# A hybrid decoder layer on one core: ACT and DVE issue ready work of the dense products before that of the mixers

## The chip, the cores and the metric

The kernel runs on one core of one Trainium2 chip. The metric is the device time of one execution in microseconds (us). Before the change the median of three runs is 1505.16 us (1505.06 to 1505.33). The engines are called PE (matrix products), PEld (its weight loads), DVE, ACT, POOL and SP (here SP issues all DMA transfers).

## What is computed

One decoder layer on 1024 tokens of width 1024, all in float32. The input is modulated, projected to 3984 columns, and the columns feed three groups of recurrent heads ("mixers"); their outputs are projected back, then comes a squared-ReLU MLP of width 4096. Cut to what matters:

```python
mod = silu(c) @ ada_w + ada_b                     # shift1, scale1, gate1, shift2, scale2, gate2
h = x * (1 + scale1) + shift1
z = h @ w_in                                      # 1024 x 1024 by 1024 x 3984
o_h = hgrn2_mixer(z_h, ...)                       # 4 heads, chunkwise gated linear attention
o_g = gla_mixer(z_g, ...)                         # 6 heads, the same with a low-rank gate
o_r = rwkv7_mixer(z_r, ...)                       # 6 heads, delta-rule recurrence
o = concatenate([o_h, o_g, o_r]) @ w_out          # 1024 x 1024
x = layer_norm(ALPHA * x + (1 + gate1) * o, ln1_g, ln1_b)
h = x * (1 + scale2) + shift2
m = square(relu(h @ mlp_w_up)) @ mlp_w_down       # 1024 x 4096, 4096 x 1024
x = layer_norm(ALPHA * x + (1 + gate2) * m, ln2_g, ln2_b)
```

## The kernel before, in words

**Blocks.** The tokens are cut into two blocks of 512 (`NB`, `NT`). `build` emits the work in this order: the input projection of block 0 (`z_block(0)`, `z_rest(0)`), the mixers of block 0 (`mix(0)`), the modulation's later sums (`ada_later`), the input projection of block 1 (`z_block(1)`, `z_rest(1)`), the output projection and layer norm of block 0 (`out_block(0)`), the last columns of block 1 (`z_last`), the MLP's input of block 0 (`mlp_moving`), the mixers of block 1 (`mix(1)`), eight MLP chunks of block 0 (`mlp_chunk`, 512 columns of the 4096 each; after the fifth of them stands `out_block(1)`), and eight of block 1, the last of them `mlp_last`.

**Dense products.** Each float32 operand is split in two float32r parts, high and low. For a weight slab of 128 rows, `slab` (L1282) loads it into a `raw` buffer, ACT casts it to `wh` (L1278 in `split`), and DVE subtracts to get `wl` (L1279). `mm3` (L1326) then issues three matmuls per pair of tiles (L1328 to L1330): high by high, high by low, low by high. This text calls one such matmul a product; there are 5040 of them. A slab gives 12 products in `prod_c` and `prod_t`, and four slabs can be held (`WB`). Results gather in the PSUM banks `dn` (pool `psd`, four of them) or later `tn` (pool `pst`), and ACT and DVE take them out: L1217 and L1218 (`shift`), L1373 and L1375 (`put`), L1478 and L1479 (`out_block`), L1499 to L1504 (squared ReLU), L1517 and L1519 (the MLP's sum). Buffers of the dense products lie in the pools `dp` and, once the mixers are over, `tp`.

**Mixers.** `mixers` runs over the four tiles of 128 tokens of a block. Each tile is a chain of small steps that alternates between DVE, ACT, PE and small transfers through DRAM: `rw_*` for the delta-rule heads (with `rw_invert`, L687 to L743, whose triangular inverses go through DRAM), `la_*` for the linear attention (`la_attn` L408 with seven levels of L417 to L438, `la_end`). Their buffers lie in the pools `mp` and `cp`, their PSUM banks `mr` and `ml` in `psm`. On PE there are 3219 issues that are not products, most of them of the mixers. The outputs go to DRAM (`oD`, L538 and L825), from where `out_block` reads them back (`from_dram` L1303, transposes L1293).

**Order.** No engine follows the order of the code. `Order` (L874) takes the recorded instructions, their dependences and buffers, and writes out one order per engine; `apply` fixes it, and on the chip each engine issues in that order, waiting where it must. `run` (L1016) plays the program through with costs by formula; when an engine is free, `pick` (L1059) chooses among the instructions that are ready by that play and whose new buffers fit (`fits`, L1050; buffers of one kind are given out in the order of the code). The choice is the lowest rank, which is the pair of a level (`self.level(n)` in `build` and `mixers`) and the place in the code. Levels: 0 for `mix(0)` and `out_block(0)`, 2 for `z_block(1)`, 3 for `ada_later`, 0, 0, 3.5, 4.5, 5.5, 6.5 for the steps of `mix(1)` (`M1`), 3, 4, 5 and so on for the MLP chunks. So within block 0 an instruction of the mixers that is ready goes ahead of one of `z_block(1)`. For PE alone `pick` has two rules ahead of the rank: products first while few columns have passed lately (`behind`, L1045), and staying in one tile mode of the array (L1078).

Of the kernel before, what the change touches and what calls it, by code (L numbers as in the profile page):

```python
# [831 lines left out]
PE, ACT, DVE, POOL, SP = ENGINES = ("PE", "Activation", "DVE", "Pool", "SP")  # L832
# [8 lines left out]

KEEP = 1.2

SWITCH, ISSUE = 130, 20
DMA_ISSUE, DMA_START, DMA_END = 500, 600, 900

# [27 lines left out]
class Order:  # L874
# [21 lines left out]
    def cost(self, n):  # L896
# [6 lines left out]
        if e == SP:  # L903
            k = 1
            for _, m in dst[0].ap:
                k *= m
            run = min(ap.ap[-1][1] if ap.ap[-1][0] == 1 else 1 for ap in (src[0], dst[0]))
            return k / run * max(0.44, max(4 * run, 512 if run > 16 else 0) / 360), 0
# [107 lines left out]
    def run(self):  # L1016
        n = len(self.ins)
# [10 lines left out]
        ready = {e: [] for e in ENGINES}  # L1028
# [12 lines left out]
        recent, self.sum = collections.deque(), 0  # L1041
        dense = [self.eng[k] == PE and self.ins[k].ins[0].bass_ap.dtype == F32R for k in range(n)]


        def behind():  # L1045
            while recent and recent[0][0] < t - HAM_TICK:
                self.sum -= recent.popleft()[1]
            return self.sum < KEEP * HAM_COLUMNS

        def fits(k):  # L1050
            want = {}
            for tag, name in (x for m in self.run_of.get(k, (k,)) for x in self.takes[m]):
                j = want.get(tag, 0)
                if used[tag] + j >= self.room[tag] or self.tags[tag][nxt[tag] + j] != name:
                    return False
                want[tag] = j + 1
            return True

        def pick(e):  # L1059
            held = []  # L1060

            def take(x):
                ready[e].remove(x)
                heapq.heapify(ready[e])
                return x[1]

            if e == PE and run:
                x = self.rank[run[0]]
                if x not in ready[e]:
                    return None  # L1070
                run.pop(0)
                return take(x)
            if e == PE and behind():
                for x in sorted(ready[e]):
                    if dense[x[1]] and fits(x[1]):
                        return take(x)

            if e == PE and self.now != (P, P):  # L1078
                for x in sorted(ready[e]):
                    if self.mode[x[1]] == self.now and fits(x[1]):  # L1080
                        run.extend(self.run_of.get(x[1], ())[1:])
                        return take(x)
            while ready[e]:
                k = heapq.heappop(ready[e])[1]
                if fits(k):
                    break
                held.append(k)
            else:
                k = None
            for x in held:  # L1090
                heapq.heappush(ready[e], self.rank[x])
            if e == PE and k is not None:
                run.extend(self.run_of.get(k, ())[1:])
            return k

        while done < n:
            for e in ENGINES:
                while idle[e] <= t:
                    k = pick(e)
                    if k is None:  # L1100
                        break
# [42 lines left out]
            t = events[0][0]  # L1144
            while events and events[0][0] <= t:
                _, what, k = heapq.heappop(events)
# [534 lines left out]
```

## Time and profile before

| | |
|---|---|
| median of 3 runs | 1505.16 us (1505.06 to 1505.33) |
| the profiled execution, its own time | 1511.53 us |
| its span, first to last instruction | 1509.7 us |
| PE busy | 1416.9 us, 94% of the span, 11226 matmuls |
| DVE busy | 1052.7 us, 70% |
| ACT busy | 708.0 us, 47% |
| DMA engines busy | 44.6% by the main queue |
| granted clock of TensorE, mean | 0.975 |

How to read it: the profiled execution is one execution with the profiler on. Times in the views are counted from the start of its span. Matmuls are pipelined: each is shown for some 0.39 us, and the next starts 0.23 us after it, so the distance of their starts is what counts. Idle time of PE is read with the wait that ended it. [...]

### The profile page before, as it was taken

The numbers are of one execution on the slowest core, as the hardware profiler recorded it, in microseconds if no ns is written. First come the engines' busy times: TensorE is split into PE (matmuls) and PEld (weight loads), VectorE is DVE, ScalarE is ACT, GpSimd is POOL, SyncE is SP. The second block draws the span as 40 slices with busy tenths as digits, with TensorE's granted clock in tenths as the row PEclk, the third lists the DMA queues.
The fourth block names the chain that finished last, engine by engine and source line by source line (L and its number), as shares of the span: only waits on it lengthen the run. The fifth ranks groups of instructions, "written<-read, shape, count | busy, mean of one in ns | idle before, by whom it ended". The sixth has DMA issues, their size and how long they took to land.

```text
span 1509.7 us, 29223 instructions
## 1 busy us (share of the span) xinstructions
PE 1416.9 (94%) x11226; PEld 1131.9 (75%) x11226; DVE 1052.7 (70%) x2130; ACT 708.0 (47%) x1527; POOL 25.4 (2%) x32
## 2 busy tenths in 40 slices
PE   6999998889899896989899999999999999999996
PEld 5878876667787675767677788787887888888884
DVE  8787479889785576979788765475569445445478
ACT  3543365677756544666657443323343323333331
POOL 1000000000000000000000000000000000000004
PEclk9999999999989997999999999999999999999998
DMA  9998662524424655142423243454336432333331
GB/s 349 331 340 290 191 191 68 164 80 142 125 86 131 197 171 190 51 133 69 122 80 89 67 153 94 143 182 155 91 93 217 144 96 93 97 93 97 94 116 56
DMA packets 163291, 214.00 MB, mean 142 GB/s; under 512 B 39856, under 2 KB 90192, under 8 KB 163152
## 3 DMA queue, kind: packets, MB, share of 16 engines
q1 hardware_dynamic: 163152, 212.14, 44.6%
q8 instruction: 88, 1.44, 0.4%
q14 instruction: 51, 0.42, 0.1%
HBM read 180.03 MB, written 32.06 MB: 140 GB/s over the span
## 4 chain that ended last, share of the span: by engine, by line
PE 47%; DVE 7%; ACT 3%; DMA 2%; issue 1%; POOL 1%; SPq 0%; DVEq 0%; ACTq 0%; POOLq 0%
PE dn L1330 10%; PE dn L1328 10%; PE dn L1329 10%; PE tn L1330 5%; PE tn L1329 5%; PE tn L1328 5%; DMA lnr<-in_ln_b_dram 1%; DVE wl L1279 1%; DMA G<-zgt 1%; PE ml L434 0%; ACT L154 0%; DVE Rs L423 0%; DVE xt L1462 0%; DVE ld L459 0%; PE tn L1293 0%
## 5 line engine op out<-in xcount | busy, mean ns | idle before, releaser
L1278 ACT CAST wh<-raw 128x512 fp32r<-128x512 f32 (+2 forms) x424 | 253.0, 599 | 538.2 <-PE dn L1330 253.3
L1279 DVE TENSOR_TENSOR wl<-raw,wh 128x512 fp32r<-128x512 f32 (+2 forms) x424 | 278.3, 661 | 303.1 <-ACT wh L1278 279.5
L1328 PE MATMUL dn<-wh,ah 128*128 128x512 f32 (+1 forms) x736 | 288.3, 395 | 10.1 <-ACT s L1373 3.4
L1329 PE MATMUL dn<-wl,ah 128*128 128x512 f32 (+1 forms) x736 | 289.9, 394 | 4.6 <-DVE wl L1279 4.6
L1330 PE MATMUL dn<-wh,al 128*128 128x512 f32 (+1 forms) x736 | 287.8, 396 | 4.5 <-DVE al L1504 4.5
L1328 PE MATMUL dn<-ah,wh 128*128 128x512 f32 x560 | 226.7, 406 | 18.6 <-ACT ah L1321 11.4
L1329 PE MATMUL dn<-al,wh 128*128 128x512 f32 x560 | 225.8, 403 | 0.0
L1330 PE MATMUL dn<-ah,wl 128*128 128x512 f32 x560 | 223.5, 402 | 0.9 <-DVE wl L1279 0.7
L1328 PEld LDWEIGHTS dn<-wh,ah 128*128 128x128 f32 x736 | 141.6, 193 | 42.2 <-ACT s L1499 5.2
L1330 PEld LDWEIGHTS dn<-wh,al 128*128 128x128 f32 x736 | 141.6, 193 | 33.2 <-DVE al L1504 6.6
L1329 PEld LDWEIGHTS dn<-wl,ah 128*128 128x128 f32 x736 | 142.3, 193 | 31.3 <-DVE wl L1279 5.3
L1328 PEld LDWEIGHTS dn<-ah,wh 128*128 128x128 f32 x560 | 106.5, 190 | 45.2 <-ACT ah L1321 11.4
L1330 PEld LDWEIGHTS dn<-ah,wl 128*128 128x128 f32 x560 | 105.7, 189 | 24.4 <-DVE wl L1279 2.0
L1329 PEld LDWEIGHTS dn<-al,wh 128*128 128x128 f32 x560 | 106.3, 190 | 22.5 <-issue 0.9
L1330 PE MATMUL tn<-ah,wl 128*128 128x512 f32 x256 | 100.8, 394 | 0.0
L1329 PE MATMUL tn<-al,wh 128*128 128x512 f32 x256 | 100.2, 391 | 0.0
L1328 PE MATMUL tn<-ah,wh 128*128 128x512 f32 x256 | 99.6, 389 | 0.0
L157 ACT ACTIVATE ld<-ld 128x320 f32<-128x320 f32 (+1 forms) x120 | 54.8, 489 | 25.7 <-DVE ld L417 17.5
L1519 DVE TENSOR_TENSOR xt<-xt,dn 128x512 f32<-128x512 f32 x104 | 64.4, 679 | 0.1
L1244 DVE SCALAR_TENSOR_TENSOR xt<-xt,xt 128x1024 f32<-128x1024 f32 x48 | 58.3, 1216 | 8.3 <-DMA xt<-in_ada_wt_dram 8.0
L1329 PEld LDWEIGHTS tn<-al,wh 128*128 128x128 f32 x256 | 48.1, 188 | 11.2
L1328 PEld LDWEIGHTS tn<-ah,wh 128*128 128x128 f32 x256 | 48.1, 188 | 10.6
(288 smaller groups left out, 1960.5 us busy)
## 6 DMA issues: line engine op xcount, KB each, us to landing
raw<-in_mlp_w_up_dram SPq DMA_DIRECT2D x128, 256.0 KB
raw<-in_mlp_w_down_dram SPq DMA_DIRECT2D x128, 256.0 KB
xt<-in_ada_wt_dram SPq DMA_DIRECT2D x48, 512.0 KB
raw<-in_w_in_dram SPq DMA_DIRECT2D x64, 256.0 KB
raw<-in_w_in_dram SPq DMA_DIRECT2D x48, 192.0 KB
raw<-in_w_out_dram SPq DMA_DIRECT2D x32, 256.0 KB
raw<-in_w_in_dram SPq DMA_DIRECT2D x32, 196.0 KB
raw<-in_xt_dram SPq DMA_DIRECT2D x24, 256.0 KB
```

The costliest lines, as they stand in the source:

```text
L157: ins = nc.scalar.activation(out, in_, func, **kw)
L1244: nc.vector.scalar_tensor_tensor(w, w, 1.0, self.cact, ALU.mult, ALU.mult, accum_out=self.sums[:, q:q + 1])
L1278: nc.scalar.copy(hi[:, 0:n], src)
L1279: (eng or nc.vector).tensor_tensor(lo[:, 0:n], src, hi[:, 0:n].bitcast(F32), ALU.subtract)
L1328: nc.tensor.matmul(ps, lh, rh, start=first, stop=False)
L1329: nc.tensor.matmul(ps, lh, rl, start=False, stop=False)
L1330: nc.tensor.matmul(ps, ll, rh, start=False, stop=last)
L1519: nc.vector.tensor_tensor(acc[t][:, cs], acc[t][:, cs], ps, ALU.add)
```

## The change

`Order.run` marks each instruction of ACT and DVE that writes or reads a buffer or bank of the pools `dp`, `psd`, `tp` or `pst` (`feeds`). When ACT or DVE is free, `pick` first takes the lowest-ranked marked instruction that is ready and fits, whatever its level; only if there is none does it choose by rank among the rest. Nothing is computed otherwise, and no buffer, tile or transfer is added or removed. The orders of PE, POOL and SP are made by the same rules as before, but follow, since what becomes ready when in the play changes.

```diff
--- before.py
+++ after.py
@@ -841,6 +841,8 @@
 
 KEEP = 1.2
 
+DENSE = ("dp", "psd", "tp", "pst")
+
 SWITCH, ISSUE = 130, 20
 DMA_ISSUE, DMA_START, DMA_END = 500, 600, 900
 
@@ -1041,6 +1043,9 @@
         recent, self.sum = collections.deque(), 0
         dense = [self.eng[k] == PE and self.ins[k].ins[0].bass_ap.dtype == F32R for k in range(n)]
 
+        feeds = [self.eng[k] in (ACT, DVE) and any(t.split("_")[-2] in DENSE for t, _ in self.uses[k])
+                 for k in range(n)]
+
 
         def behind():
             while recent and recent[0][0] < t - HAM_TICK:
@@ -1064,6 +1069,10 @@
                 heapq.heapify(ready[e])
                 return x[1]
 
+            if e in (ACT, DVE):
+                for x in sorted(ready[e]):
+                    if feeds[x[1]] and fits(x[1]):
+                        return take(x)
             if e == PE and run:
                 x = self.rank[run[0]]
                 if x not in ready[e]:
```

Lines of the classes below stand nine further down in the changed kernel: L1278 becomes L1287, L1293 becomes L1302.

The order on ACT, around the casts of four slabs of `z_block(1)` (`wh_1032` to `wh_1041`, L1278 and L1287). Before, they stand in the mixers' last tile (tile 3: `ld_746`, `ld_752`, `sm_734`), and between two casts come five to ten other instructions:

```order
L1278 CAST wh_1032_5796<-raw_1031_5794 128x392
L157 ACTIVATE ld_746_4447<-ld_746_4447 128x5x64
L782 COPY UV_670_3873<-mr_735_4351 64x3x64
...
L157 ACTIVATE ld_749_4467<-ld_749_4467 128x10x32 x2
L1278 CAST wh_1035_5814<-raw_1034_5812 128x392
L517 COPY sc_1631<-ml_748_4454 64x6x64
...
L777 COPY sm_738_4382<-mr_737_4375 128x192
L157 ACTIVATE ld_752_4487<-ld_752_4487 128x20x16 x2
```

After, they stand in tile 2 (`ld_678`, `wk_631`), with two or four instructions between them:

```order
L1287 CAST wh_1032_5796<-raw_1031_5794 128x392
L157 ACTIVATE wk_627_3508<-wk_625_3501 128x384
L580 ACTIVATE wk_631_3522<-wk_610_3434,oka_1627,vcols_524 128x128
L1287 CAST wh_1035_5814<-raw_1034_5812 128x392
L580 ACTIVATE wk_631_3522<-wk_610_3434,oka_1627,vcols_524 128x128 x2
L1287 CAST wh_1038_5832<-raw_1037_5830 128x392
L1382 COPY s2_1023_5778<-dn_995_5630 128x392
L157 ACTIVATE ld_678_3901<-ld_678_3901 128x5x64
```

The same casts have moved up by about one tile of the mixers.

The order on PE at the end of `mix(0)`. Before, its last issue (L497) stands among the products of `z_block(1)`, and the 96 products of `z_rest(1)` are still to come ahead of `out_block(0)`:

```order
L1329 MATMUL dn_5792<-wl_5887,ah_4968 128x392
L497 MATMUL ml_4709<-V_4181,ld_4693 64x64 x10
L1330 MATMUL dn_5792<-wh_5886,al_4969 128x392
...
L1264 MATMUL ml_4751<-consts,mod 8x128
L1328 MATMUL dn_5950<-ah_4843,wh_5956 128x512
```

After, the last product of `z_rest(1)` (`dn_5953`) stands ahead of the last two of the five small levels of tile 3's `la_attn` (L434), and no product comes until `out_block(0)` transposes what it read back (L1302):

```order
L1339 MATMUL dn_5953<-ah_5018,wl_6083 128x512
L434 MATMUL ml_4581<-Rs_4579,ld_4574 32x32 x20
L434 MATMUL ml_4610<-Rs_4608,ld_4603 32x32 x20
L446 MATMUL ml_4632<-Qz,K_4180 32x64 x20
L471 MATMUL ml_4671<-st,ld_4659 128x128
...
L497 MATMUL ml_4709<-V_4181,ld_4693 64x64 x10
L1273 MATMUL ml_4751<-consts,mod 8x128
...
L1302 MATMUL dn_6112<-consts,raw_6110 128x128 x4
```

The dense work of block 1's projection, which ran beside the whole of `mix(0)` and past its end, now ends before `mix(0)` does: 99 issues of mixers and modulation stand without a product between them.

## Rows read from the trace of the kernel before

**Rows 1.** The page: busy time of each engine, share of the span, instructions.

```profile
PE 1416.9 (94%) x11226; PEld 1131.9 (75%) x11226; DVE 1052.7 (70%) x2130; ACT 708.0 (47%) x1527; POOL 25.4 (2%) x32
```

**Rows 2.** Stages: start:end, length, busy (instructions) by engine, granted clock, DMA, GB/s.

```profile
203.00:470.00 267.00, 245.39 (x3524) 190.81 (x3524) 218.29 (x527) 178.67 (x453) 0.00 (x0) 0.96 0.39 119
470.00:607.00 137.00, 119.04 (x574) 92.74 (x573) 87.18 (x178) 67.04 (x132) 1.86 (x2) 0.90 0.58 179
607.00:890.00 283.00, 264.15 (x3581) 202.63 (x3581) 236.71 (x536) 176.29 (x432) 0.00 (x0) 0.98 0.29 86
```

**Rows 3.** The same view of a stretch with products alone.

```profile
1178.00:1444.00 266.00, 266.00 (x1153) 216.18 (x1151) 126.23 (x197) 85.94 (x144) 0.00 (x0) 1.00 0.32 98
```

**Rows 4.** Waits of PE, 203:470: waiting line, releaser, us, times, longest.

```profile
PE dn L1328 <- DVE s L1218: 4.5, 4, 2.5
...
PE dn L1328 <- ACT s L1373: 1.4, 1, 1.4
```

**Rows 5.** Timeline of ACT, 389:408: start, us, engine, line, operation, names, shapes, count.

```profile
390.70 0.52 ACT L1278 CAST wh<-raw 128x392 fp32r<-128x392 f32 x1
...
404.47 0.51 ACT L1278 CAST wh<-raw 128x392 fp32r<-128x392 f32 x1
```

**Rows 6.** The view of rows 2 for two stretches around it.

```profile
395.00:408.00 13.00, 9.23 (x63) 8.30 (x63) 6.72 (x15) 11.89 (x31) 0.00 (x0) 0.99 0.62 167
408.00:425.00 17.00, 17.00 (x223) 14.13 (x223) 8.98 (x21) 8.36 (x22) 0.00 (x0) 0.50 0.31 95
```

**Rows 7.** Waits of PE, 607:890.

```profile
PE dn L1328 <- ACT s L1499: 2.1, 2, 1.3
...
PE dn L1330 <- DVE al L1504: 1.7, 3, 1.3
```

**Rows 8.** Timeline of DVE, 441:465, the end of the mixers of block 0.

```profile
440.88 0.81 DVE L423 TENSOR_TENSOR Rs<-ld,Qz 128x640 f32<-128x640 f32 x1
...
445.47 0.56 DVE L1279 TENSOR_TENSOR wl<-raw,wh 128x392 fp32r<-128x392 f32 x1
...
448.77 1.04 DVE L1279 TENSOR_TENSOR wl<-raw,wh 128x392 fp32r<-128x392 f32 x2
...
454.07 1.04 DVE L1279 TENSOR_TENSOR wl<-raw,wh 128x392 fp32r<-128x392 f32 x2 [1.47 <-ACT wh L1278]
...
459.78 0.68 DVE L1279 TENSOR_TENSOR wl<-raw,wh 128x512 fp32r<-128x512 f32 x1
462.93 0.83 DVE L537 TENSOR_TENSOR o<-o,ms 128x640 f32<-128x640 f32 x1
```

**Rows 9.** Timeline of SP, 462:505: the mixers' last store and a read-back.

```profile
463.78 0.33 SPq L538 DMA_DIRECT2D oD<-o  x1
...
498.11 0.36 SPq L1305 DMA_DIRECT2D raw<-oD  x1
```

**Rows 10.** Timeline of SP, 889:893: the same pair for block 1.

```profile
890.03 0.33 SPq L538 DMA_DIRECT2D oD<-o  x1
...
892.33 0.38 SPq L1305 DMA_DIRECT2D raw<-oD  x1
```

**Rows 11.** Chain that ended last, in order of time: a transfer in it.

```profile
659.82 5.03 DMA G<-zgt
```

**Rows 12.** Timeline of PE, 500:509: the first products of the output projection.

```profile
508.11 1.22 PE L1328 MATMUL dn<-wh,ah 128*128 128x512 f32 x2 [1.40 <-ACT wh L1278]
```

**Rows 13.** Waits of PE, 470:607.

```profile
PE dn L1293 <- DVE s L1300: 5.9, 2, 4.8
PE dn L1329 <- DVE wl L1279: 4.6, 1, 4.6
```

**Rows 14.** Waits of ACT, 203:470 (first row) and 607:890.

```profile
ACT wh L1278 <- PE dn L1330: 8.2, 7, 4.4
...
ACT wh L1278 <- PE dn L1330: 33.3, 16, 3.4
```

**Rows 15.** Timeline of ACT, 413:437: one such wait.

```profile
419.64 0.52 ACT L1278 CAST wh<-raw 128x392 fp32r<-128x392 f32 x1 [4.42 <-PE dn L1330]
```

## The prediction

> **What bounds the kernel now.** I read the page first. PE is busy for 94% of the span, DVE for 70%, ACT for 47% [rows 1], so PE sets the time, and what a change in order can give lies in the remaining 6% and in stretches at the lower clock. Where products run alone, 1153 of them take 266 us [rows 3]: 0.231 us each, with nothing lost. From 890 us on the kernel looks like that, and the built order of PE is the same before and after for the last 2368 issues. Up to 203 us the input projection of block 0 fills PE, and product 860 comes after 67 other issues in both orders. So only three stages can move [rows 2]: 203 to 470 (mixers of block 0 beside the projection of block 1), 470 to 607 (output projection, layer norm), 607 to 890 (mixers of block 1 beside MLP chunks). In the first, 600 products at 0.231 are 139 us; the other 128 us go to 1484 other issues, so one of these costs 0.087 us with its waits.
>
> The view of waits says why PE stands still in the first stage. Its products wait for what takes banks empty: 4.5 us for DVE's L1218 and 1.4 for ACT's L1373 [rows 4]. [...] ACT casts a weight slab at 390.70 and the next at 404.47 [rows 5], while it is busy with mixers for 11.89 of 13 us; PE is busy for only 9.23 of these 13, and the clock is 0.50 for the 17 us behind [rows 6]. A slab is 12 products, 2.8 us of PE; 13.8 us without one starves it. This is the spot that the change aims at.
>
> **The change part by part.** Nothing is added or removed; instructions move. All counts here are of the built orders.
>
> *Feeding PE in the first stage, a gain.* With casts and emptied banks ahead of the mixers, the products' waits (5.9 us) should nearly all go: I take 5. Of the 21 us at the low clock at most half, 10.5, can come back, since PE was busy in the large piece; part of that piece was mixers, which wait for DVE at either clock. I take 7. Sum 12, bounds 0 (the low clock only moves) and 16.4.
>
> *The same in the third stage.* [...] I take 7, bounds 0 and 9.3.
>
> *The end of the mixers of block 0, a cost.* Before, product 1392, the last of z_block(1), comes after all 1545 issues up to the mixers' last, and the 96 products of z_rest(1) (22 us) cover the way from the mixers' last store to the output projection. After, all 96 are issued while 90 of these issues are still to come, and nothing is left to cover that way. How long is it? From the end of the third small level's Rs at 441.7 to the mixers' store at 463.78 is 22.1 us [rows 8, 9]; DVE's L1279 in it takes 3.3, casts and products between the steps some more, so I take 17 (13 to 22). Store to read-back: 2.3 us, the gap that block 1 shows [rows 10]. The transfer: 5 us, the length of one on the chain [rows 11], 3 at best. From the sixth read-back, which must wait until a first `raw` buffer is free, to the first product it was 10.0 us [rows 9, 12]. Together 34 us (28 to 41). In that time PE has 99 issues and 32 transposes, 131 at 0.087 or 11 us. It loses 23 (17 to 30). Before, PE is idle for 18 us of the second stage [rows 2], and 10.5 of these lie elsewhere in it [rows 13]; of the other 7.5 I count 5 at this place, one piece of them the 1.4 us of [rows 12]. The low clock behind the gap is there already, 0.90 over the stage [rows 2]. Net cost: 18 by these middles; I take 15, nearer the low end, because DVE and ACT work for the mixers alone there, and keep 12 and 25.
>
> *Steps that stay behind.* Before, PE had made 1611 other issues when out_block(0) began; after it is 1555, so 56 issues of block 1's first tile, 4.9 us, come later, together with the DVE steps in front of them. They fall to where PE waits for the layer norm and its slab, 5.9 and 4.6 us [rows 13]. I take a gain of 2, bounds 0 and 4.9. DVE's later sums for the modulation go ahead of mixers too, at 60 to 160 us, and cost nothing: products of block 0 cover them, and PE's place in the mixers is the same at product 860.
>
> *The end of the mixers of block 1.* They end at product 2634 instead of 2449, with 102 products (23.6 us) behind them before out_block(1). Their way to its transposes is some 12 us: the 2.3 of [rows 10], the 5 of [rows 11], and a handful of DVE and ACT steps the size of L537's 0.83 [rows 8], say 5. So it is covered, with 11 us to spare, and costs nothing; were the cover gone, it would cost what block 0's end costs.
>
> *Sum.* -12 - 7 + 15 - 2 = -6 us on the profiled execution's own 1511.5 us, so 1505.5. That execution is 6.4 us above the median of the runs; taken off the median, 1505.2 - 6 = **1499**.
>
> **The rivals.** *Starved at the output projection (slower).* If DVE's dense work delays the mixers themselves, the gap grows. DVE is busy for 218 of 267 us in the stage [rows 2]. The 102 dense splits of z_block(1) and z_rest(1) that go ahead are about 60 us at 0.52 to 0.68 us each [rows 8]; before, 94 of them ran when the mixers left DVE free. If half of that time now stands in the chain, the store comes at 463.8 + 30 = 494 and the first product of out_block(0) 17 us later, at 511 instead of 508; with 56 issues (4.9) still owed and the third stage gaining nothing, the time is up by 8, at two thirds by 18. I put it at 1518, between the two. It decides at a first product later than 508. For it speaks how far the mixers lag: at product 1360 the order has 1095 other issues behind it, not 1535. Against it: DVE's idle 49 us in the stage take up some.
>
> *A cast that waits holds the mixers behind it (slower).* ACT issues in order. Its casts already waited for PE to free a `wh` buffer: 8.2 us in the first stage, 33.3 in the third [rows 14], 4.4 of it in one place [rows 15]. Before, they stood where the mixers had little ready; now ready steps stand behind them. If that much comes again in front of mixers, block 0's end is 8.2 us later (-6 + 8 = +2), and block 1's 33, of which 11 are covered: 22 more lost, +24. I put it at 1518, halfway between. [...]
>
> *No difference.* In the third stage the casts wait for PE, not PE for them, so products are fed already; gains and cost cancel: 1505.
>
> *A larger gain.* All clock and waits return and the gap is at its low bound: -16 - 9 + 12 - 5 = -18, or 1487.
>
> That the rule does nothing is out: the casts stand a tile earlier in the order.
>
> **How the numbers follow.** About 0.2%, 3 us, is what a measurement of this kernel can tell from no change. Forecast (1490 to 1502) 0.42, larger gain 0.08, no difference 0.18, starved 0.20, held casts 0.12. So faster 0.50, same 0.18, slower 0.32. The range reaches from the larger gain's 1487 to just above the slower cases' middle, 1520; the outer halves of these two, about 0.14, and what lies under 1487 are left out. The faster cases alone span 1487 to 1502.
>
> **What would show it.** Right: in the stage from 203 us no stretch at the low clock before the products run out; no 14 us between two casts; a gap of 28 to 41 us between the last product of z_rest(1) and the first of out_block(0) with the low clock in it; that first product at 495 to 506; the mixers of block 1 ending some 40 us later than 890, and products at 0.231 us on both sides of out_block(1). Wrong: a first product of out_block(0) later than 508, PE waiting for transposes near product 2736, or ACT's waits for PE at L1287 well above those of [rows 14] with the mixers' steps late behind them.

## The result, and the profile after

The changed kernel takes 1483.7 us (median; 1482.9 to 1487.0), against 1505.2 us for the kernel before on the same chip: ratio 0.985, 95% interval 0.983 to 0.987. It is faster by 21.5 us. The prediction was 6 us, with a range that ended at 1487: the sign was right, the size was more than three times too small.

The page of the changed kernel, busy time by engine, against [rows 1]: the work is the same, and PE is busy 11 us less.

```profile
PE 1406.1 (95%) x11226; PEld 1124.2 (76%) x11226; DVE 1055.1 (71%) x2130; ACT 708.9 (48%) x1527; POOL 25.4 (2%) x32
```

To compare kernels, I cut each trace at the same three products, whose order is the same in all of them: the first of `z_block(1)`, the first of MLP chunk 0 and the first of `out_block(1)`. The stretches are called start, first part (it holds the mixers of block 0, the gap behind them and the output projection) and MLP part (the mixers of block 1 beside MLP chunks). For the changed kernel, in the columns of [rows 2]; the first part is two rows, cut at the first product of `out_block(0)`:

```profile
0.00:209.00 209.00, 187.76 (x916) 156.91 (x917) 150.05 (x320) 88.23 (x182) 4.17 (x12) 0.98 0.84 283
209.00:502.40 293.40, 270.46 (x3651) 212.56 (x3649) 227.76 (x540) 192.57 (x475) 0.00 (x0) 0.95 0.43 129
502.40:591.40 89.00, 80.53 (x412) 64.14 (x412) 62.96 (x110) 40.34 (x73) 1.87 (x2) 0.94 0.59 184
591.40:930.00 338.60, 330.10 (x3915) 255.28 (x3914) 287.35 (x644) 212.75 (x508) 0.00 (x0) 1.00 0.37 106
930.00:1485.20 555.20, 537.27 (x2339) 435.34 (x2337) 326.99 (x520) 175.00 (x291) 19.37 (x18) 0.99 0.37 116
```

The kernel before, cut at the same products:

```profile
0.00:203.40 203.40, 187.44 (x916) 157.15 (x916) 147.38 (x318) 87.50 (x182) 4.17 (x12) 0.98 0.86 291
203.40:508.10 304.70, 278.66 (x3753) 215.55 (x3752) 241.37 (x589) 200.57 (x506) 0.00 (x0) 0.96 0.42 125
508.10:600.70 92.60, 79.07 (x326) 62.96 (x326) 57.42 (x101) 39.08 (x67) 1.86 (x2) 0.89 0.61 192
600.70:956.30 355.60, 335.95 (x3897) 261.00 (x3896) 278.89 (x605) 205.71 (x483) 0.00 (x0) 0.98 0.32 97
```

The start is 5.6 us longer, the first part 14.9 shorter (397.3 to 382.4), the MLP part 17.0 shorter, the rest 1.8 longer. The first part's figure flatters: that execution of the kernel before lay 6.4 us above its median, and six kernels below that have the same order there (runs 2, 5, 6, 7, 9 and 12) take 389.5 to 391.2 us. Against their mean, 390.4, the first part won 8.0.

The MLP part won most. Its length minus PE's busy time is PE's idle time: 355.60 - 335.95 = 19.65 before, 338.60 - 330.10 = 8.50 after, so 11.2 of the 17.0 us; the other 5.9 are busy time, at a clock of 1.00 instead of 0.98. (In the traces of these two kernels the granted clock is 1.00 or 0.50, and products of 512 columns start 0.43 us apart at 0.50 (before, 509.98 to 512.97 us) and 0.23 at 1.00. The low clock means 0.50 throughout.) Of the idle time, 14.3 us stood ahead of issues of the mixers and 5.3 ahead of products before; 4.9 and 3.6 after. Waits of PE in this part of the changed kernel, the three largest (the first and third are products, compare [rows 7]):

```profile
PE dn L1337 <- ACT ah L1511: 1.8, 2, 1.5
PE ml L488 <- DVE o L480: 1.7, 3, 0.6
PE dn L1337 <- DVE xt L1528: 1.2, 1, 1.2
```

Around the end of block 0's mixers it went as described. The store and the first read-back on SP (compare [rows 9]), then the first products of the output projection on PE (compare [rows 12]):

```profile
486.62 0.34 SPq L538 DMA_DIRECT2D oD<-o  x1
...
488.82 2.57 SPq L1314 DMA_DIRECT2D raw<-oD  x5
```

```profile
464.88 0.40 PE L1339 MATMUL dn<-ah,wl 128*128 128x512 f32 x1
...
502.39 0.96 PE L1337 MATMUL dn<-wh,ah 128*128 128x512 f32 x3 [0.34 <-ACT wh L1287]
```

The last product of `z_rest(1)` starts at 464.88, so 37.5 us pass without a product; forecast 34 (28 to 41). The stretch, and the piece of it at the low clock; the view counts 223 matmuls where the prediction counts 131 issues, because most issues of the mixers show as two matmuls in the trace (some 190 for the 99; the 32 transposes show as 32):

```profile
465.30:502.40 37.10, 22.23 (x223) 18.01 (x223) 18.12 (x34) 19.68 (x46) 0.00 (x0) 0.59 0.50 154
468.20:495.50 27.30, 17.94 (x166) 14.85 (x166) 10.75 (x22) 14.14 (x35) 0.00 (x0) 0.50 0.39 113
```

And the casts of slabs on ACT in the projection of block 1 (compare [rows 5], where two are 13.8 us apart): the longest distance between two casts there is now 10.3 us, between these two, and the next longest 7.5.

```profile
419.03 0.62 ACT L1287 CAST wh<-raw 128x512 fp32r<-128x512 f32 x1
...
429.36 0.61 ACT L1287 CAST wh<-raw 128x512 fp32r<-128x512 f32 x1
```

### The profile page after: what moved, and what is told of

The parts are those of the page before. It is cut to its first block, busy times and chain, and to the rows that moved or that the text cites. A ratio compares the mean times of both kernels' runs of the same rounds, so it can differ in the third digit from the quotient of the medians.

```text
span 1485.2 us, 29273 instructions
## 1 busy us (share of the span) xinstructions
PE 1406.1 (95%) x11226; PEld 1124.2 (76%) x11226; DVE 1055.1 (71%) x2130; ACT 708.9 (48%) x1527; POOL 25.4 (2%) x32
## 4 chain that ended last, share of the span: by engine, by line
PE 51%; DVE 4%; DMA 3%; ACT 2%; issue 1%; POOL 1%; SPq 0%; DVEq 0%; ACTq 0%; POOLq 0%
PE dn L1339 11%; PE dn L1338 11%; PE dn L1337 10%; PE tn L1338 5%; PE tn L1337 5%; PE tn L1339 5%; DMA lnr<-in_ln_b_dram 1%; PE ml L434 1%; DVE wl L1288 1%; DMA zht<-s 1%; DMA x1D<-xt 0%; DMA G<-zgt 0%; PE mr L598 0%; ACT wh L1287 0%; DVE xt L1471 0%
## 5 line engine op out<-in xcount | busy, mean ns | idle before, releaser
L1287 ACT CAST wh<-raw 128x512 fp32r<-128x512 f32 (+2 forms) x424 | 253.5, 599 | 500.4 <-PE dn L1339 215.9
L1337 PE MATMUL dn<-wh,ah 128*128 128x512 f32 (+1 forms) x736 | 284.6, 390 | 8.5 <-ACT s L1382 3.9
L1339 PE MATMUL dn<-wh,al 128*128 128x512 f32 (+1 forms) x736 | 283.4, 390 | 3.8 <-DVE al L1513 3.8
L1338 PEld LDWEIGHTS dn<-al,wh 128*128 128x128 f32 x560 | 105.8, 189 | 22.2 <-issue 0.5
L1253 DVE SCALAR_TENSOR_TENSOR xt<-xt,xt 128x1024 f32<-128x1024 f32 x48 | 58.4, 1220 | 14.6 <-DMA xt<-in_ada_wt_dram 14.5
L1339 PEld LDWEIGHTS tn<-ah,wl 128*128 128x128 f32 x256 | 48.2, 188 | 11.2
```

The costliest lines, as they stand in the source:

```text
L1253: nc.vector.scalar_tensor_tensor(w, w, 1.0, self.cact, ALU.mult, ALU.mult, accum_out=self.sums[:, q:q + 1])
L1287: nc.scalar.copy(hi[:, 0:n], src)
L1337: nc.tensor.matmul(ps, lh, rh, start=first, stop=False)
L1338: nc.tensor.matmul(ps, lh, rl, start=False, stop=False)
L1339: nc.tensor.matmul(ps, ll, rh, start=False, stop=last)
```

## The experiments

All start from the changed kernel, except the seventh. Where a rule holds for a part of the code alone, `self.at` has the place in the code at which that part begins: "ada" for `ada_later`, "z1" for `z_block(1)`, "zr1" for `z_rest(1)`, "out0" for `out_block(0)`, "mlp" for the first MLP chunk. The table has all of them; in the texts quoted below the MLP part is sometimes called the MLP stage or the third stage. "Without a product" is the longest time between the starts of two products in the MLP part, except the 5 to 6 us of the transposes ahead of `out_block(1)`, which all have. The lengths are those of one profiled execution each. The runs were timed on several chips; each ratio is to the kernel before on the same chip.

| kernel | start | first part | MLP part | PE idle in it at mixers, at products | without a product | median us | ratio to before (95%) |
|---|---|---|---|---|---|---|---|
| before | 203.4 | 397.3 | 355.6 | 14.3, 5.3 | 11.3 | 1505 to 1506.5 | 1 |
| changed | 209.0 | 382.4 | 338.6 | 4.9, 3.6 | 3.8 | 1483.7 | 0.983 to 0.987 |
| 1 ahead of the MLP | 207.5 | 384.8 | 363.0 | 16.0, 5.9 | 11.8 | 1509.4 | 1.001 to 1.004 |
| 2 MLP only | 203.8 | 390.9 | 336.1 | 3.4, 1.4 | 2.8 | 1486.0 | 0.985 to 0.987 |
| 3 ACT only | 205.6 | 397.4 | 349.2 | 10.2, 4.4 | 8.6 | 1506.2 | 0.999 to 1.001 |
| 4 DVE only | 208.0 | 373.9 | 342.9 | 6.7, 3.6 | 3.5 | 1480.1 | 0.981 to 0.984 |
| 5 DVE's splits, MLP | 203.9 | 389.8 | 356.5 | 10.7, 6.7 | 11.2 | 1504.3 | 0.997 to 1.001 |
| 6 DVE's others, MLP | 205.4 | 391.2 | 358.2 | 14.4, 4.7 | 12.5 | 1513.0 | 1.003 to 1.006 |
| 7 mixers later | 202.5 | 389.5 | 354.4 | 14.8, 2.5 | 13.8 | 1505.4 | 0.997 to 1.000 |
| 8 DVE, no modulation | 201.4 | 373.7 | 341.5 | 5.6, 3.9 | 3.5 | 1475.4 | 0.977 to 0.982 |
| 9 DVE's rows broken | 203.1 | 390.9 | 339.8 | 6.8, 4.0 | 4.5 | 1490.3 | 0.988 to 0.991 |
| 10 as 8, and ACT in the MLP | 203.5 | 373.5 | 342.3 | 5.6, 3.2 | 3.6 | 1475.8 | 0.978 to 0.982 |
| 11 as 10, products kept | 201.7 | 381.9 | 336.0 | 4.9, 1.4 | 7.0 | 1479.7 | 0.981 to 0.985 |
| 12 PE's order alone | 202.4 | 390.0 | 366.5 | 5.2, 20.0 | 5.0 | 1514.5 | 1.004 to 1.007 |

**1 and 2: which part of the program.**

```diff
         feeds = [self.eng[k] in (ACT, DVE) and any(t.split("_")[-2] in DENSE for t, _ in self.uses[k])
+                 and k < self.at["mlp"]
                  for k in range(n)]
```

> The rule holds only for instructions ahead of the MLP in the code. Of the 24.5 us between the two profiled executions, 17.0 lie between the start of the first MLP chunk and out_block(1). If the stages add, this kernel keeps the 11.3 and 3.6 us won ahead of the MLP and the 5.6 lost at the start, and has the third stage of before: about 9 us below before, 1494 to 1499 us, third stage 353 to 358 us. Rival (one shift carries through: what block 1's mixers had not issued early is what fills the third stage): the third stage is shortened here too, under 347 us, and the time is below 1490.

The second has `k >= self.at["mlp"]` in that place.

> The rule holds only for instructions of the MLP chunks and later. If the stages add: start and first stage as before (203 and 305 us), third stage 336 to 342 us instead of 355.6, the time 1486 to 1491 us, below the changed kernel if its 5.6 us at the start are real. Rival (the third stage's gain needs the later start of block 1's mixers): third stage over 347 us, time over 1495.

The MLP part of the first, then of the second, in the columns of [rows 2]:

```profile
592.30:955.30 363.00, 341.12 (x3915) 265.19 (x3913) 286.95 (x643) 214.34 (x507) 0.00 (x0) 0.97 0.33 98
```

```profile
594.70:930.80 336.10, 331.25 (x3897) 257.07 (x3897) 280.64 (x605) 204.85 (x483) 0.00 (x0) 0.99 0.35 102
```

The MLP alone gives 20 of the 21.5 us, with the first part and the start as before. Ahead of the MLP the rule won 6 us in the first part, but lost 4 at the start, and the MLP part behind it became 7 us longer than 356 (the mean of the kernel before and of runs 5 to 7, which gain nothing there: 355.6, 356.5, 358.2, 354.4). So the first run, 3 us slower than before, bears out neither line of its expectation: the parts don't simply add. Why the MLP part grew isn't settled. Its idle time is 2 us above that of before and its clock 0.97.

**3 and 4: which engine.**

```diff
+                 and self.eng[k] == ACT
```

> The rule holds on ACT alone. My prediction's reading (late casts on ACT starve the products) wants at least half of the gain here: 1495 us or less. Rival (DVE's share decides, since the low part of a slab is a DVE step and PE's order hardly moves by ACT's rule): within 3 us of before, 1502 to 1508, with the waits of PE in the third stage near 19 us as before.

> The rule holds on DVE alone. If ACT's late casts were the cause: 1495 to 1505 us, and gaps of over 10 us between two casts in the first stage as before. If DVE's share decides: 1481 to 1490 us, PE idle in the third stage 8 to 11 us instead of 19.7, products up to 468 us without a stretch at the low clock.

ACT's share alone gives nothing that can be measured in the time, DVE's alone all, and 4 to 5 us more than both (3.6 by the medians, 4.8 by the ratios). The idea that late casts on ACT are the main cause is out. By parts ACT's rule isn't quite without effect: the MLP part is 7 us shorter than 356, but the first part 7 longer than 390.4. The latter has some 42 us at the low clock in that execution, as much as the profiled execution of the kernel before, so it may be scatter. The MLP part, for ACT alone and for DVE alone:

```profile
603.00:952.20 349.20, 334.67 (x3897) 259.80 (x3896) 279.51 (x605) 205.65 (x483) 0.00 (x0) 0.98 0.34 99
```

```profile
581.90:924.80 342.90, 332.58 (x3913) 256.97 (x3911) 285.29 (x638) 209.55 (x497) 0.00 (x0) 0.99 0.35 102
```

PE's waits with ACT alone, 14.5 us, are below the 19 that were expected, at a time that is the same; and even with ACT's rule two casts of the MLP part are 18.9 us apart, so it isn't ACT's choice that holds them up. With DVE alone the distance between two casts in the first part went up to 19.9 us once, with no more than 4.8 us without a product anywhere in the projection; a piece of 3.4 us at the low clock, at 354 us, is the one sign in the text that did not fit.

**5 and 6: which of DVE's steps.**

```diff
+                 and self.eng[k] == DVE and k >= self.at["mlp"]
+                 and self.ins[k].outs[0].bass_ap.dtype == F32R
```

> The rule holds only for DVE's splits of the MLP (the low parts of weights and of the squared ReLU, outputs in float32r). If an early low part is what lets PE go on: the MLP stage (first product of chunk 0 to the last of out_block(1)) shrinks from 423 us to 400 to 408, the time is 1484 to 1490. Rival (splits and the emptying of banks only work together, since PE's order has the same 2150, 2535 and 2921 other issues at the chunks' ends as before): 1502 to 1508 us.

(These counts, and those of the seventh run's text, include 96 products of block 0 that I had taken for other issues.) The sixth has `!= F32R`.

> The rule holds only for DVE's other steps of the MLP (sums that empty the banks, squares, residual and layer norm). If the emptying of banks alone is the cause: MLP stage 400 to 408 us, 1484 to 1490. Rival (only both together): 1502 to 1508 us, MLP stage 419 to 427.

Neither gives the gain. The fifth still has two stretches of 11.2 us without a product; PE's waits name the low part of the squared ReLU first:

```profile
PE dn L1347 <- DVE al L1521: 5.4, 3, 1.8
```

That low part takes two steps of DVE: a square in float32 (L1520 in both kernels) and the subtraction behind it (L1521). Of the two, the fifth rule marks only the subtraction, the sixth only the square. In the first stretch of the fifth run (631.0 to 642.2 us) the square stands late, and the subtraction right behind it; in that of the sixth (from 635.6 us) the square comes early, and the subtraction 13 us after it:

```profile
640.68 0.67 DVE L1520 TENSOR_TENSOR s<-s 128x512 f32<-128x512 f32 x1
...
641.41 0.68 DVE L1521 TENSOR_TENSOR al<-s,ah 128x512 fp32r<-128x512 f32 x1
```

```profile
632.86 0.68 DVE L1520 TENSOR_TENSOR s<-s 128x512 f32<-128x512 f32 x1
...
645.98 1.28 DVE L1521 TENSOR_TENSOR al<-s,ah 128x512 fp32r<-128x512 f32 x2
```

So each rule left one half of the same chain behind. What the emptying of banks adds to the low parts, no run shows apart.

The sixth is 7 us slower; the loss lies behind the MLP part (561.0 us from there to the end, 553.4 before), and what happens there wasn't followed up.

**7: is it only that the mixers end later?** An edit of the kernel before:

```diff
-M1 = (0, 0, 3.5, 4.5, 5.5, 6.5)
+M1 = (0, 0, 4.5, 5.5, 6.5, 7.5)
```

> The kernel before, with the levels of block 1's mixers one higher from the second tile on, so they run one MLP chunk later, as densely among the products as before (some 380 other issues per 192 products), and no rule on DVE. Theory of slack (the rule thins the mixers out among the products, 270 to 330 issues in chunks 1 and 2 instead of 384, so their steps wait less): nothing gained, PE still waits 15 us or more at the mixers' steps in the MLP stage, 1500 to 1508 us. Rival (the mixers only had to end later, closer to out_block(1)): half the gain or more, 1495 us or less.

No: nothing is won, PE waits 14.8 us at the mixers' steps as before, and stretches of 13.8, 11.3 and 8.8 us without a product remain. The number fits the theory of slack, but the second run had already spoken against that theory: its mixers stand as densely among the products of chunks 0 and 1 as before (360 and 362 other issues, before 377 and 386), and it has the whole gain. (In chunk 2 it does have fewer, 318 against 402.) Run 9 below has the counts of before in every chunk and most of the gain. So not the density.

**8: the loss at the start.**

```diff
+                 and self.eng[k] == DVE and not self.at["ada"] <= k < self.at["z1"]
```

> The rule on DVE alone, but not for the later sums of the modulation. If these sums, waiting for their transfers ahead of ready work, cost the 4 to 6 us at the start: the first product of z_block(1) comes at 179 to 182 us instead of 184.4, and the time is 1474 to 1478 us. Rival (the start's loss is in the emptying of banks or only scatter of one execution): 1479 to 1482 us.

It was the modulation's sums. With PE's issues at the same places as in run 4, the start is 6.6 us shorter and the time 4.8 us (4 by the ratios). The start takes 207.5 to 209.0 us in the three kernels whose DVE puts these sums first (changed, 1 and 4), and 201.4 to 205.6 in all others. (The 184.4 us of the text above belong to a product 96 ahead of the first of `z_block(1)`; it came at 178.1.) DVE's wait for the sums' transfers up to 210 us, in the changed kernel and in this one (8.0 us in the kernel before):

```profile
DVE xt L1253 <- DMA xt<-in_ada_wt_dram: 14.5, 9, 5.6
```

```profile
DVE xt L1260 <- DMA xt<-in_ada_wt_dram: 9.4, 8, 2.9
```

**9 and 12: DVE's long rows, or PE's order?** The stretches without a product led to this pair. The kernel before in its longest one, by engine as in [rows 2]:

```profile
640.00:650.00 10.00, 7.06 (x182) 5.98 (x182) 9.79 (x30) 6.54 (x14) 0.00 (x0) 1.00 0.13 41
```

PE there, from the last mixers' issue that goes on at once to the first product:

```profile
641.47 0.92 PE L807 MATMUL mr<-UV,E 128*64 128x64 f32 x24
643.76 0.46 PE L471 MATMUL ml<-st,ld 128*128 128x128 f32 x2 [1.37 <-DVE ld L459]
...
647.83 0.94 PE L640 MATMUL mr<-cen,zm 128*128 128x128 f32 x6 [0.81 <-DVE bon L626]
649.51 0.55 PE L665 MATMUL mr<-consts,BK 128*128 128x128 f32 x3 [0.75 <-DVE bon L635]
...
650.84 1.22 PE L1330 MATMUL dn<-wh,al 128*128 128x512 f32 x2 [0.24 <-DVE al L1504]
```

DVE, the last step of the mixers and the first three of the products:

```profile
649.38 0.81 DVE L463 TENSOR_TENSOR ld<-ld,K 128x640 f32<-128x640 f32 x1
650.11 0.68 DVE L1504 TENSOR_TENSOR al<-s,ah 128x512 fp32r<-128x512 f32 x1
650.71 0.68 DVE L1503 TENSOR_TENSOR s<-s 128x512 f32<-128x512 f32 x1
651.32 0.68 DVE L1279 TENSOR_TENSOR wl<-raw,wh 128x512 fp32r<-128x512 f32 x1
```

DVE is busy for 9.79 of 10 us, with steps of the mixers alone, and PE follows it step by step. The steps that PE's next products need stand behind this row, though what they read had been there for more than 11 us. By the order of the steps, the low part at 650.11 reads a square that DVE made at 636.65, the square at 650.71 had only to wait for ACT's step at 636.10, and the low part of weights at 651.32 a cast that ACT had issued by 638.24:

```profile
636.65 0.65 DVE L1503 TENSOR_TENSOR s<-s 128x512 f32<-128x512 f32 x1
```

```profile
636.10 0.63 ACT L1502 ACTIVATE ah<-s 128x512 fp32r<-128x512 f32 x1
```

A row of the mixers is not harmful as such: run 4 has rows of 16.4 and 14.4 us without a step for the products on DVE, and no stretch over 3.5 us without a product on PE. By its rule such a row comes only where no step for the products is ready in the planner's play; before, they were left behind.

Run 9 only keeps such steps from being left behind for long; `self.fed` is the time in the play at which DVE last took a marked step, and the rule holds on DVE in the MLP:

```diff
-            if e in (ACT, DVE):
+            if e == DVE and t - self.fed > BURST:      # BURST = 4000
                 for x in sorted(ready[e]):
                     if feeds[x[1]] and fits(x[1]):
                         return take(x)
```

> The kernel before, with one addition: in the MLP, DVE takes a ready dense step ahead of the mixers only if it has issued none for 4 us in the planner's play. PE's order keeps its place (2055, 2441, 2850 and 3155 other issues ahead of chunks 1 to 4, as before). If DVE's long rows of mixer steps as such make the stretches without a product on PE: the three of 8 to 11 us before out_block(1) go, the MLP part falls from 356 to under 345 us, the time is 1495 or less. Rival (PE's order has to carry products between the mixers' steps, and that comes only where dense steps always go first): 1500 to 1508, stretches of over 8 us remain.

Run 12 turns it round: the planner makes PE's order with the rule on DVE in the MLP, then plans again with that order held and no rule.

```diff
-        self.run()
+        left = dict(self.left)
+        self.run()
+        self.left = left
+        self.run(list(self.order[PE]))
...
+            if e == PE and fixed:
+                x = self.rank[fixed[nth]] if nth < len(fixed) else None
+                if x not in ready[e] or not fits(x[1]):
+                    return None
+                nth += 1
+                return take(x)
+            if e in (ACT, DVE) and not fixed:
```

> The planner runs twice: first with the rule on DVE in the MLP, then with that order of PE held fixed and no rule, so DVE picks by rank again. If PE's order carries the gain: 1484 to 1490, as with the rule in the MLP alone, no stretch of over 6 us without a product on PE between 600 and 920 us. Rival (DVE's precedence itself is needed, or PE waits for low parts that DVE makes too late): 1495 or more, with PE's waits for DVE's L1279 steps well above those of before.

The MLP part, run 9 and then run 12, and two of run 12's waits of PE:

```profile
594.00:933.80 339.80, 328.98 (x3897) 257.52 (x3896) 279.06 (x605) 206.06 (x483) 0.00 (x0) 0.99 0.34 101
```

```profile
592.40:958.90 366.50, 341.32 (x3898) 261.85 (x3897) 280.58 (x605) 206.69 (x483) 0.00 (x0) 0.96 0.32 94
```

```profile
PE dn L1356 <- DVE al L1530: 12.0, 4, 3.5
...
PE dn L1356 <- DVE wl L1305: 2.2, 1, 2.2
```

Run 9 has PE's issues at the same chunk ends as before and three quarters of the gain, 15.9 us. Its DVE in the place that corresponds (three of the steps that now stand in the row):

```profile
634.21 0.68 DVE L1522 TENSOR_TENSOR s<-s 128x512 f32<-128x512 f32 x1
...
638.31 0.69 DVE L1523 TENSOR_TENSOR al<-s,ah 128x512 fp32r<-128x512 f32 x1
...
642.15 0.68 DVE L1522 TENSOR_TENSOR s<-s 128x512 f32<-128x512 f32 x1
```

Run 12 has the rule's order on PE, waits little at the mixers' steps (5.2 us), but 20.0 us ahead of products, most of it for the low part of the squared ReLU (L1530), not, as the text above has it, for the splits of weights: 8 us slower than before. Its longest stretch without a product is only 5.0 us, of the size of those in the kernels that gain (2.8 to 7.0), and yet PE's idle time is 25 us against 19.6 before: the same lack, spread over more waits. So PE's order alone doesn't carry the gain; DVE's has to change, and PE's then follows.

**10 and 11: what is left.** Run 10 adds ACT in the MLP to run 8:

```diff
+                 and (self.eng[k] == DVE or k >= self.at["mlp"])
+                 and not self.at["ada"] <= k < self.at["z1"]
```

> The rule on DVE without the modulation's sums, and on ACT in the MLP alone. If the parts add (first part 374 us as with DVE alone, MLP part 336 to 339 as with both engines, start 201 to 204): 1469 to 1474 us. If ACT's share gives nothing in the MLP either: 1473 to 1478, as without it.

ACT's share gives nothing here either. Run 11 keeps 48 products of `z_rest(1)` for the stretch behind the mixers:

```diff
+        last = max(k for k in range(n) if self.eng[k] == PE and k < self.at["ada"])
+        held = [k for k in range(n) if self.eng[k] == PE and self.at["zr1"] <= k < self.at["out0"]]
+        for k in held[-48:]:
+            self.after[k].setdefault(last, 0)
```

> As the kernel just above, but in the planner's play the last 48 products of z_rest(1) (11 us) wait for the last issue of block 0's mixers on PE. My prediction priced the stretch without products at some 23 us of PE for 34 us, of which 11 us of products would win back 6 to 9: first product of out_block(0) as early, 5 us or more below the kernel above. Rival (the products are missed as much amid the mixers as at their end): within 3 us of it.

The first part, 201.7 to 583.6 us:

```profile
201.70:583.60 381.90, 351.62 (x4078) 277.62 (x4078) 297.64 (x689) 240.34 (x572) 1.86 (x2) 0.95 0.48 146
```

It is 8.4 us longer than in run 10. The first product of `out_block(0)` comes as early (491.1 against 490.2), but the stretch of 21.5 us without a product is now two, of 18.6 and 9.6. The MLP part behind it is 6.3 shorter, and the time 3.9 longer, which is neither what the text hoped for nor its rival. The stretch of 18.6 us lies amid the mixers, from 450.3 us, so the products were missed there. But up to the first product of `out_block(0)` that cost only 2.7 of the 8.4 us (289.4 against 286.7); the other 5.7 lie behind it, where the stretch without a product ahead of the MLP is 17.8 us instead of 13.3. Why that one grew wasn't followed up.

The fastest is run 8: 1475.4 us (1473.0 to 1479.3), ratio 0.977 to 0.982. Run 10 can't be told from it.

## Why the prediction was wrong in size and right in sign

- **"The same in the third stage. I take 7, bounds 0 and 9.3": this step failed.** The MLP part won 17.6 us against the mean of 356.2, outside its bounds, and the rule there alone 20. No run shows the 7 or the 9.3. They were my estimate, from the products' waits for the squared ReLU, 2.1 and 1.7 us [rows 7], and half of the time at the low clock, which in the trace of before is 10.2 us between 607 and 890 us. The step took the mixers' share of PE as fixed, by 0.087 us an issue "with its waits". But 14.3 of the 19.6 us of idle time stood ahead of mixers' issues, and 9.4 of them went. In a list of waits by line they are spread over a dozen lines of at most 2.1 us each; seen over time, half of them (7.1 us) lie in three stretches, at 639.6, 721.6 and 803.8 us, of 11.3, 8.7 and 8.4 us without a product, in which DVE is busy for 28.0 of 28.4 us; the low clock, 0.50, stands behind the first and the third (650.2 to 653.6 and 814.0 to 820.8 us). The other half is spread over the part. I had found their like in the first stage ([rows 5] and [rows 6]), and looked for no more of them in the third. Runs 4, 9 and 12 show what stood behind them: the order of DVE, whose long rows of mixer steps left the products' steps behind. The two casts around the first stretch, which the text would have taken for its cause:

```profile
638.24 0.61 ACT L1278 CAST wh<-raw 128x512 fp32r<-128x512 f32 x1
...
658.58 0.60 ACT L1278 CAST wh<-raw 128x512 fp32r<-128x512 f32 x1
```

- **The cause it named, ACT's casts, was the wrong engine.** "The spot that the change aims at" was read from ACT's timeline. By runs 3 and 4 ACT's order is worth nothing in the sum; the late casts were a sign of the same lack, not its source. Two things that the text did not look at spoke against its reading. In the same trace ACT makes no cast for 29.9 us from 233.9 us on, and PE is busy there for 26.45 of 30 us, at a clock of 1.00 (first line below). And the low clock behind the 13.8 us without a cast was mostly that one execution's: the six kernels with the same order there have two casts 13.8 to 14.1 us apart at that place too, but 0 to 6.8 us at the low clock instead of 17. The view from 390 to 432 us, in the kernel before (second line) and in run 7 (third):

```profile
234.00:264.00 30.00, 26.45 (x535) 20.03 (x533) 27.96 (x84) 16.68 (x43) 0.00 (x0) 1.00 0.23 70
...
390.00:432.00 42.00, 36.84 (x405) 30.73 (x405) 27.11 (x59) 28.88 (x74) 0.00 (x0) 0.80 0.42 121
```

```profile
390.00:432.00 42.00, 35.73 (x590) 29.51 (x589) 32.23 (x68) 31.74 (x83) 0.00 (x0) 1.00 0.42 123
```

- **Feeding PE in the first stage, 12, and the cost of the gap, 15, with 2 back.** The parts can't be measured apart, but their sum can: +1 by the text, -8.0 measured. The gap itself came as worked out, 37.5 us with the low clock in it (0.50 from 468.2 to 495.5 us), and the first product of `out_block(0)` at 502.4 lies within 495 to 506. PE was idle for 14.9 us of the gap; of its 22.2 busy us about half goes to the low clock, if 131 issues at 0.087 are 11.4. By that price the gap cost 26 us, where the text had 23. (The upper end of its length, 41, doesn't follow from its terms, which give 39.) The gain was too small: ahead of the gap PE's idle time fell by some 14 us (21.8 to 8.0), where the text had 5 of waits, and behind it by 5 (13.5 to 8.5), where it had 2. That no low clock would be left ahead of the gap came true: it is 1.00 from 209 to 464.9 us. The 21 us at the low clock that the text starts from are in the trace of before two pieces at 0.50, 291.8 to 295.2 and 407.8 to 424.9 us, together 20.5. No run shows apart how much of them came back; half at most was my estimate, and the distances of products, 0.43 us at the low clock and 0.23 at 1.00, fit it. Run 8, with a gap of only 22 us, has the first part at 373.7.
- **Startup, 0: wrong by 5.5 us.** The later sums of the modulation were to "cost nothing". The sums that go ahead wait for their transfers, 14.5 us instead of 8.0, and ready work stands behind them. Run 8 without them gets the start back (201.4 us against 208.0 in run 4). So steps that wait did hold ready steps behind them, as the rival of held casts had it for ACT, but on DVE and at the start.
- **The end of block 1's mixers, 0: right**, though the mixers' last store comes 19 us later than before (909.27 against 890.03), not some 40: the MLP part is shorter by 17.
- **The rival of held casts did not come.** That a cast can hold ACT the trace of before shows: for 4.42 us ahead of the cast at 419.64 [rows 15] ACT did nothing else. But ACT's waits of casts for PE in the MLP part fell from 60.3 + 27.7 to 34.2 + 16.3 us:

```profile
ACT wh L1287 <- PE dn L1339: 34.2, 19, 3.3
ACT wh L1287 <- PE dn L1338: 16.3, 10, 3.4
```

- **The rival of no difference** rested on the sentence that casts wait for PE, so products are fed already. Both hold: casts waited 88 us over the whole part, and in three places PE had no product for 8 to 11 us. A sum over a stage does not exclude either.

With the measured terms (start, first part, MLP part and the rest, each against the mean of the kernels that gain nothing there): +5.5 - 8.0 - 17.6 + 1 = -19 us on the profiled execution, which lay 3.3 us above its own median; so -22, where the medians show -21.5.

## What to carry to other kernels

Where one engine prepares work for the matrix engine and also runs a chain of small steps, look in its order for long rows of chain steps that leave ready preparing steps behind, and break those rows. Of a stage with waits, don't only sum the waits by line: list the longest times between two products too, and see what every other engine did in them. A rule that puts work first should leave out steps that wait for transfers, and it is worth trying on each engine and each part alone. A stretch at the low clock in one profile should be looked for in a second execution before a sum is built on it.

## What the runs showed that was not expected

The same order gives 389.5 to 391.2 us in the first part in six profiled executions, and 397.3 in the one that the prediction was read from: a single profile can be off by 2% in one part, as much as most terms of the sum. The clock goes with it: that part had some 43 us at the low clock in the one execution and 26 to 36 in the six. And the 131 issues of the gap cost twice what the text's price gives: 22.2 busy us at a mean granted clock of 0.59, where 0.087 us an issue would be 11.4. That the clock is the reason isn't shown apart, since the price is a mean over other issues; but the gap's transposes (L1302) follow each other at 0.213 us at the low clock, and at 0.109 us where it is 1.00.
